# Two buffers outside the stages of a hybrid encoder block, in place of address pads

## The chip, the cores and the metric

The kernel runs on one core of a Trainium2 chip. The metric is the time of one execution on the device, in microseconds; several executions are taken and their median is given. The profile is of one more execution.

## The reference

One layer of a streaming encoder, for 512 tokens of width 1024, in float32. Only what the kernel's order of work needs is shown:

```python
h = rms_norm(x, norm_mix)
u_pool, u_lru, q, k, v, g_logits = split(h @ w_in)      # 5 x 1024 columns, and 3 x 1024 gate logits
gates = sigmoid(g_logits + b_gate)                      # 3 branches
y_pool = pool_mixer(u_pool)     # windows 2, 4, 8, 16: mean minus token, a 256x256 map, a scale
y_lru  = rglru_mixer(u_lru)     # conv of width 4, two gates, a linear recurrence over tokens
y_sb   = stick_breaking_attention(rms_norm(q), rms_norm(k), v)   # 8 heads of 128, causal
merged = sum(gates[i] * (y_i @ w_branch[i]) for the three branches)
x  = x + merged @ w_out
h2 = rms_norm(x, norm_ffn)
x  = x + (silu(h2 @ w_ffn_gate) * (h2 @ w_ffn_up)) @ w_ffn_down     # 2816 columns
```

## The kernel before, in words

Every product is made of three TensorE matmuls on operands split in a high and a low part (high x high, high x low, low x high). A weight piece of 128 x 1024 is loaded into a `raw` buffer, copied by ScalarE to `whi` (line 141) and subtracted by VectorE to `wlo` (line 142); there are three buffers of each in the pool `wp`. `weights` keeps about three pieces made ahead, at a priority 200 ahead of the place where they are emitted (`AHEAD`). Large products are done as seven half-size products instead of eight, in the order 11, 12, S2, S1, S3, S4, 22 (`ORDER`, and `product`, line 321, with moving operands of 256 columns).

The work is written as Python closures that are handed out during the matmuls: `tick` (line 363) takes one task from the list `abg` (attention) and one from `bg` (the rest). `half_chunk` calls `tick` after every twelve matmuls of a chunk. A planner then fixes the order on each engine from the order of emission, moved ahead by `tc.high_priority(n)`; each engine and each DMA queue (SP's, ACT's, and POOL's) works its list in order.

The stages that matter here, in order of time:

- **Start.** `warm` is filled with ones (line 335) and multiplied nine times (`WARM`, line 458) while the first loads arrive.
- **First stage** (pool `ap0`, tags `w`, `t` and `b` with 8, 8 and 13 buffers of 4 KB per partition): norm, gates of branches 0 and 1, the recurrence, then v, k, q (`tok_product`, line 837) which are stored by POOL's queue to DRAM (`qd`, line 790), then the gate of branch 2 as two units `cc` of seven products each (lines 894 to 920). A unit's two results `gx`, `gy` (line 895) are stored to `gd2` by POOL's queue (`gate_done`, line 892).
- **Mixing stage** (pools `sp`, `ap1`, `pmm`, `paux`): the pool `sp` takes the bytes of `ap0` and has 30 slots `s` and 12 slots `l` for loads, each 2 KB per partition. A tile waits for whatever last used its own bytes. `pmm` has three PSUM banks for chunk results, `paux` three for the attention and the pooling map.
  - Four pooling chunks in the order 1, 0, 3, 2 (`POOL`). Each leaves two banks, which ScalarE empties into slots (`evac_u`, line 981, results `up`). `pool_mean` (VectorE) and `pool_back` (TensorE, bank `pps`) follow as `bg` tasks, `pool_back` one chunk later.
  - Then four branch chunks of the recurrence (`ps_br`), then four of the pooling branch.
  - Beside these runs attention (`head_tasks`): for head h, `load` of q, k and v (`at`, line 1052, on SP's queue) at position 5h of `abg`, `trans` (eight transposes `pq`, line 1059, then copies `qkh`, `qkl`) at 5h+3, `vsplit` at 5h+4, three `scores` (`z`, `K`, `A`, `E`) at 5h+5, 5h+7 and 5h+9, `wtrans` (ten transposes `pw`, line 1109, in three banks, then `wth`, `wtl`) at 5h+12, and `yout` (`py`) at 5h+14.
- **Last branch, output product, FFN.** All with seven-product pieces except the first chunks; the products of `product` and of `piece` (line 1661) use moving operands of 256 columns.

Three things in the code of before are only about addresses. `PAD` is an unused tile of 41 floats. The `whi` and `wlo` buffers are 1152 floats long for a content of 1024, and a piece starts at an offset `o`: 0 for the pieces of ordinary chunks, and in the seven-product stages `STEPS` (0, 4, 8, 12) for the first four pieces and `OFF` (16) for all that follow. `warm` is as wide as the 512 columns that are multiplied.

```python
tx, ty = b4([2, S], f"gx{cc}"), b4([2, S], f"gy{cc}")     # tag "b"
...
def evac_u(ps, name):
    u = slot(name)
    act(two(u), in_order(ps), AF.Copy)
    return u
...
load_pool_weights(0)
queue_attention()
for g in POOL:
    pool_chunk(g)
```

Of the kernel before, what the change touches and what calls it, by code (L numbers as in the profile page):

```python
# [16 lines left out]
P = 128  # L17
S = 512
# [15 lines left out]
AHEAD = 200  # L34
PAD = 41


OFF = 16
STEPS = (0, 4, 8, 12)
NAW, NAT, NAB = 8, 8, 13  # L40
# [27 lines left out]
def layer_kernel(ctx: ExitStack, tc: tile.TileContext, x, xt, vecs, w_in, w_qkv7, w_gate7, w_pool, w_rg, w_ig,  # L68
# [6 lines left out]
    mp = ctx.enter_context(tc.tile_pool(name="mp", bufs=4))  # L75
    wp = ctx.enter_context(tc.tile_pool(name="wp", bufs=3))
    late = ctx.enter_context(ExitStack())
    hstack = ctx.enter_context(ExitStack())
# [50 lines left out]

    def weight_tiles(nh, nl, o=0):  # L130
        return [wp.tile([P, 1024 + 128], F32R, tag=tag, name=n)[:, o:o + 1024]
                for tag, n in (("whi", nh), ("wlo", nl))]

    def split_w(raw, shape, n, o=0):
        hi, lo = weight_tiles("whi" + n, "wlo" + n, o)
        if len(shape) == 3:
            hi, lo = (t.rearrange("p (a b) -> p a b", a=shape[1]) for t in (hi, lo))
        else:
            hi, lo = (t.rearrange("p (a b c) -> p a b c", a=shape[1], b=shape[2]) for t in (hi, lo))
        with tc.high_priority(60):  # L140
            act(hi, raw, AF.Copy)  # L141
            dve.tensor_tensor(lo, raw, hi.bitcast(F32), ALU.subtract)  # L142
        return hi, lo
# [58 lines left out]
    def add_seven(un, nm, i):  # L202
# [3 lines left out]
        def make(n):  # L206
            if nm == "S4":
                r = qraw[u, "12", i]
                dve.tensor_tensor(r, r, qraw[u, "S2", i], ALU.add)
            src = qraw[u, {"S1": "21", "S3": "11", "S4": "12"}.get(nm, nm), i]  # L210
            o = 0
            if u >= 3:
                o = goffs.pop(0) if goffs else OFF
            parts = split_w(src, [P] + list(shape), n, o)
            if nm == "11":
                qraw[u, "S2", i] = r = b4(list(shape), f"qs{u}{i}")
                dve.tensor_tensor(r, qraw[u, "21", i], src, ALU.add)
# [12 lines left out]
    goffs = list(STEPS)  # L230

# [28 lines left out]
    BNEXT = {"11": ("21", BY), "S1": ("11", BX), "S2": ("12", BX)}  # L260
    boffs = list(STEPS)

# [3 lines left out]
    def add_branch7(u, nm):  # L266
        def make(n):
# [3 lines left out]
            else:  # L271
                t = (BY if nm in ("11", "S3") else BX)[u]
            parts = split_w(t, [P, 2, 4, P], n, boffs.pop(0) if boffs else OFF)
            if nm in BNEXT:
# [57 lines left out]

    cst.tile([P, PAD], F32, tag="pad", name="pad")
    warm = cst.tile([P, S], BF16, tag="warm", name="warm")
    dve.memset(warm, 1.0)
# [108 lines left out]
    with ExitStack() as first:  # L444
# [12 lines left out]
        for i in range(WARM):  # L457
            nc.tensor.matmul(wps[:, 0, :], warm[:, 0:P], warm, start=True, stop=True)

# [434 lines left out]
        for cc in range(2):  # L894
            tx, ty = b4([2, S], f"gx{cc}"), b4([2, S], f"gy{cc}")
            if cc:
# [48 lines left out]
    with ExitStack() as mix:  # L945
# [34 lines left out]

        def evac_u(ps, name):
            u = slot(name)
            act(two(u), in_order(ps), AF.Copy)  # L983
            return u
# [35 lines left out]
        def pool_chunk(g):  # L1020
            pss = chan_chunk(("pool", g), hn, 1)
            us = [evac_u(pss[j], f"up{g}{j}") for j in range(2)]
            for j in range(2):
# [20 lines left out]
        def head_tasks(h):  # L1044
# [4 lines left out]
            def load():  # L1049
                for t in range(3):  # L1050
                    r = slot_ld(f"at{h}{t}", (NS, HD))
                    nc.sync.dma_start(r, qd[t, g][:, hd].rearrange("(b p) c -> p b c", p=P))
                    st["raw", t] = r
# [119 lines left out]
        def queue_attention():  # L1173
# [8 lines left out]
            for p in range(max(todo) + 1):  # L1182
                abg.append(lambda fs=todo.get(p, ()): [f() for f in fs])

        load_pool_weights(0)
        queue_attention()
        for g in POOL:
# [110 lines left out]
    with ExitStack() as ffn:  # L1298
# [114 lines left out]
        made = [0, NDIRECT]  # L1413
        offs = []

# [13 lines left out]
        def make_a(upto):  # L1429
            while made[0] < min(upto, len(steps)):  # L1430
                c, nm = steps[made[0]]
                made[0] += 1
                if (c, nm) == (NDIRECT, "11"):
                    offs.extend(STEPS)
                while made[1] < min(c + 2, DOWN):
# [5 lines left out]
        def split_a(src, n):  # L1441
            o = offs.pop(0) if offs else OFF
            h, l = (t.rearrange("p (w k c) -> p w k c", w=2, k=4)
                    for t in weight_tiles("wh" + n, "wl" + n, o))
            act(h, src, AF.Copy)  # L1445
# [133 lines left out]
        def make_d(upto):  # L1579
            while dmade[0] < min(upto, len(dsets)):  # L1580
                nm, n = dsets[dmade[0]]
                dmade[0] += 1
                if dmade[0] == 1:
                    offs.extend(STEPS)
                dfetch(dmade[0])
# [156 lines left out]
```

## Time and profile before

| What | us |
|---|---|
| median of 3 timed runs | 871.64 |
| lowest and highest of them | 871.51, 872.29 |
| the profiled execution, its own time | 872.32 |
| its span, first to last instruction | 870.5 |
| TensorE busy | 860.6 |
| VectorE busy | 741.1 |
| ScalarE busy | 523.1 |
| GpSimd busy | 91.2 |

The mean granted TensorE clock is 1.000. A row of the timeline has the start, the length (both in us, from the start of the span), the engine (a q behind it means the engine's queue, which issues), the line, the operation, what is written and read, the shapes and the count; in brackets stands how long the engine was idle before it and what released it. PE is TensorE, DVE VectorE, ACT ScalarE, POOL GpSimd, SP SyncE. A row of the waits has the total, the number of times and the longest.

### The profile page before, as it was taken

The page shows a single profiled execution, that of the slowest core. Times are in us where ns is not written, and L with a number is a line of the kernel's source. Part 1 is how long each engine was busy: PE and PEld are TensorE (multiplying, and loading weights), DVE is VectorE, ACT ScalarE, POOL GpSimd, SP SyncE. Part 2 cuts the span into 40 slices and gives each one's busy share as a digit, 9 for nine tenths or more (in the row PEclk, how much of TensorE's full clock was granted, in tenths as well). Part 3 has the DMA queues.
Part 4 walks back from the last instruction along what each step waited for, and adds up shares of the span by engine and source line. Part 5 has one row for each costly group of instructions (what it writes and reads, how often), then busy time and mean ns, then how long its engine had stood idle before and what let it go on. Part 6 is the DMA issues. An engine that isn't in the chain of part 4 may idle for free.

```text
span 870.5 us, 14271 instructions
## 1 busy us (share of the span) xinstructions
PE 860.6 (99%) x5563; PEld 790.0 (91%) x5563; DVE 741.1 (85%) x961; ACT 523.1 (60%) x727; POOL 91.2 (10%) x130
## 2 busy tenths in 40 slices
PE   9999999999999999999999999999999999999998
PEld 7888878888899888889889998889999999999998
DVE  7899897998796599977988786699998888899974
ACT  7554989557966565565665545464555555755642
POOL 1110002232433101000001100000000000121200
PEclk9999999999999999999999999999999999999999
DMA  9586356798582886644636955345543433797913
GB/s 339 165 287 203 98 167 187 212 324 253 178 275 73 241 243 203 221 122 151 214 103 167 199 172 169 98 139 151 156 111 97 116 104 119 228 240 194 196 42 121
DMA packets 116643, 154.08 MB, mean 177 GB/s; under 512 B 8160, under 2 KB 90080, under 8 KB 116576
## 3 DMA queue, kind: packets, MB, share of 16 engines
q1 hardware_dynamic: 103904, 107.30, 38.4%
q0 software_dynamic: 12528, 45.62, 22.0%
q8 instruction: 43, 0.70, 0.3%
q10 hardware_dynamic: 144, 0.26, 0.1%
q14 instruction: 24, 0.20, 0.1%
HBM read 132.71 MB, written 18.87 MB: 174 GB/s over the span
## 4 chain that ended last, share of the span: by engine, by line
PE 84%; DVE 7%; ACT 5%; DMA 2%; issue 1%; SPq 0%; ACTq 0%; DVEq 0%
PE ps_y L321 11%; PE ps_x L321 8%; PE ps_q L837 7%; PE ps_dy L1661 6%; PE ps_dx L1661 5%; PE ps_br L312 3%; PE ps_br L313 3%; PE ps_br L314 3%; PE ps_bY L1280 2%; PE ps_gate L740 2%; PE ps_gy L321 2%; DVE wlo L142 2%; PE ps_bX L1280 2%; PE ps_gx L321 2%; PE ps_lru L312 1%; PE ps_out L312 1%
## 5 line engine op out<-in xcount | busy, mean ns | idle before, releaser
L141 ACT ACTIVATE whi<-raw 128x1024 fp32r<-128x1024 f32 x69 | 72.9, 1056 | 78.3 <-PE ps_out L313 16.1
L142 DVE TENSOR_TENSOR wlo<-raw,whi 128x1024 fp32r<-128x1024 f32 x69 | 84.3, 1221 | 24.8 <-ACT whi L141 24.3
L142 DVE TENSOR_TENSOR wlo<-qw,whi 128x1024 fp32r<-128x1024 f32 x48 | 58.4, 1220 | 16.5 <-ACT whi L141 16.3
L141 ACT ACTIVATE whi<-qw 128x1024 fp32r<-128x1024 f32 x48 | 50.6, 1054 | 28.8 <-PE ps_q L837 14.8
L1445 ACT ACTIVATE wh_S<-w_S 128x1024 fp32r<-128x1024 f32 x36 | 38.2, 1062 | 30.2 <-PE ps_y L321 18.3
L1565 POOL DMA_DIRECT2D dw<-in_w_down_dram x20 | 17.0, 864 | 306.1 <-DMA dw<-in_w_down_dram 263.8
L1446 DVE TENSOR_TENSOR wl_S<-w_S,wh_S 128x1024 fp32r<-128x1024 f32 x36 | 43.9, 1221 | 3.2 <-ACT wh_S L1445 3.2
L1445 ACT ACTIVATE wh<-w 128x1024 fp32r<-128x1024 f32 x27 | 28.6, 1060 | 29.3 <-PE ps_x L321 9.1
L1446 DVE TENSOR_TENSOR wl<-w,wh 128x1024 fp32r<-128x1024 f32 x27 | 33.0, 1221 | 8.2 <-ACT wh L1445 8.2
L1445 ACT ACTIVATE whdS<-dw 128x1024 fp32r<-128x1024 f32 x20 | 21.2, 1061 | 20.3 <-PE ps_dy L1661 11.2
L1096 DVE TENSOR_TENSOR_SCAN E<-K,ahead 128x512 f32<-128x512 f32 (+3 forms) x32 | 25.4, 814 | 3.9 <-ACT K L1092 3.9
L1446 DVE TENSOR_TENSOR wldS<-dw,whdS 128x1024 fp32r<-128x1024 f32 x20 | 24.2, 1222 | 4.9 <-ACT whdS L1445 4.9
L312 PE MATMUL ps_br<-yHH,whi 128*128 128x512 f32 x64 | 24.6, 385 | 1.4 <-ACT up L983 1.4
L312 PE MATMUL ps_lru<-HH,whi 128*128 128x512 f32 x64 | 24.6, 384 | 0.0
L312 PE MATMUL ps_br<-yph,whi 128*128 128x512 f32 x64 | 24.5, 383 | 0.0
L312 PE MATMUL ps_pool<-HH,whi 128*128 128x512 f32 x64 | 24.5, 383 | 0.0
L312 PE MATMUL ps_gate<-HH,whi 128*128 128x512 f32 x64 | 24.4, 381 | 0.0
L313 PE MATMUL ps_lru<-HL,whi 128*128 128x512 f32 x64 | 24.3, 379 | 0.0
L314 PE MATMUL ps_lru<-HH,wlo 128*128 128x512 f32 x64 | 24.3, 379 | 0.0
L313 PE MATMUL ps_gate<-HL,whi 128*128 128x512 f32 x64 | 24.3, 379 | 0.0
L314 PE MATMUL ps_gate<-HH,wlo 128*128 128x512 f32 x64 | 24.3, 379 | 0.0
L313 PE MATMUL ps_pool<-HL,whi 128*128 128x512 f32 x64 | 24.3, 379 | 0.0
(740 smaller groups left out, 3444.5 us busy)
## 6 DMA issues: line engine op xcount, KB each, us to landing
raw<-in_w_in_dram SPq DMA_DIRECT2D x31, 512.0 KB, 5.3
qw<-in_w_qkv_dram SPq DMA_DIRECT2D x24, 512.0 KB, 6.8
dw<-in_w_down_dram POOLq DMA_DIRECT2D x20, 512.0 KB, 9.2
w<-in_w_ffn_gate_dram SPq DMA_DIRECT2D x36, 256.0 KB, 3.7
w<-in_w_ffn_up_dram SPq DMA_DIRECT2D x36, 256.0 KB, 4.2
raw<-in_w_branch_dram SPq DMA_DIRECT2D x16, 512.0 KB, 3.9
qw<-in_w_qkv_dram POOLq DMA_DIRECT2D x12, 512.0 KB, 8.1
qd<-r POOLq DMA_DIRECT2D x12, 512.0 KB, 6.7
```

The source lines that it names most:

```text
L141: act(hi, raw, AF.Copy)
L142: dve.tensor_tensor(lo, raw, hi.bitcast(F32), ALU.subtract)
L312: nc.tensor.matmul(ps, lh, rh, start=start, stop=False, skip_group_check=skip)
L313: nc.tensor.matmul(ps, lh, rl, start=False, stop=False, skip_group_check=skip)
L314: nc.tensor.matmul(ps, ll, rh, start=False, stop=stop, skip_group_check=skip)
L321: nc.tensor.matmul(o, a_[a][:, w, k, :], il2(b_[b][:, k, :]), start=first and n == k == 0, stop=last and n == 2 and k == 3, skip_group_che ...
L837: nc.tensor.matmul(ps[:, a, :], b_[:, k, ts_], il(a_[:, kk, :]), start=first and n == k == 0, stop=n == 2 and k == 3, skip_group_check=True)
L1096: dve.tensor_tensor_scan(E[:, c0:c0 + n][:, ::-1], K[:, c0 + 1:c0 + n + 1][:, ::-1], ahead[:, S - n:][:, ::-1], 0.0, ALU.mult, ALU.add)
L1280: nc.tensor.matmul(o, ah[x_][:, w, k, :], il2(b[k][y_]), start=first_ and n == k == 0, stop=n == 2 and k == 3, skip_group_check=True)
L1445: act(h, src, AF.Copy)
L1446: dve.tensor_tensor(l, src, h.bitcast(F32), ALU.subtract)
L1661: nc.tensor.matmul(o, a_[a][:, w, k0 + k, :], il2(b_[b][:, k, :]), start=first and i == k == 0, stop=last and i == 2 and k == nk - 1, skip ...
```

## The change

A pool `ex` with two buffers of 512 floats is opened beside `wp`, outside all stages. Head 0's q and k are loaded into them, at priority 400 ahead; later the last pooling chunk's two copies `up` use the same two buffers, at priority 300 ahead (`EARLY`). `queue_attention` now runs before `load_pool_weights(0)`, and the first task of its list, head 0's load, is taken off and run there; so each later attention task comes at one tick less. The second gate unit's `gx`, `gy` take buffers of tag `w` instead of `b`. `PAD`, `OFF` and `STEPS` go, the weight buffers are 1024 floats long and every piece starts at their beginning. `warm` has 128 columns and is read four times over by a broadcast.

```diff
+    ex = ctx.enter_context(tc.tile_pool(name="ex", bufs=2))
...
-    def weight_tiles(nh, nl, o=0):
-        return [wp.tile([P, 1024 + 128], F32R, tag=tag, name=n)[:, o:o + 1024]
+    def weight_tiles(nh, nl):
+        return [wp.tile([P, 1024], F32R, tag=tag, name=n)
...
-            o = 0
-            if u >= 3:
-                o = goffs.pop(0) if goffs else OFF
-            parts = split_w(src, [P] + list(shape), n, o)
+            parts = split_w(src, [P] + list(shape), n)
...
-            parts = split_w(t, [P, 2, 4, P], n, boffs.pop(0) if boffs else OFF)
+            parts = split_w(t, [P, 2, 4, P], n)
...
-    cst.tile([P, PAD], F32, tag="pad", name="pad")
-    warm = cst.tile([P, S], BF16, tag="warm", name="warm")
+    warm = cst.tile([P, P], BF16, tag="warm", name="warm")
...
-            nc.tensor.matmul(wps[:, 0, :], warm[:, 0:P], warm, start=True, stop=True)
+            nc.tensor.matmul(wps[:, 0, :], warm, warm.unsqueeze(1).to_broadcast([P, 4, P]), start=True, stop=True)
...
-            tx, ty = b4([2, S], f"gx{cc}"), b4([2, S], f"gy{cc}")
+            tx, ty = (b4([2, S], f"g{n}{cc}", "bw"[cc]) for n in "xy")
...
-        def evac_u(ps, name):
-            u = slot(name)
-            act(two(u), in_order(ps), AF.Copy)
+        def evac_u(ps, name, last):
+            u = ex.tile([P, S], F32, tag="u", name=name) if last else slot(name)
+            with tc.high_priority(EARLY if last else 0):
+                act(two(u), in_order(ps), AF.Copy)
             return u
...
-            us = [evac_u(pss[j], f"up{g}{j}") for j in range(2)]
+            us = [evac_u(pss[j], f"up{g}{j}", g == POOL[3]) for j in range(2)]
...
                 for t in range(3):
-                    r = slot_ld(f"at{h}{t}", (NS, HD))
-                    nc.sync.dma_start(r, qd[t, g][:, hd].rearrange("(b p) c -> p b c", p=P))
+                    with tc.high_priority(400 if h == 0 and t < 2 else 0):
+                        r = (ex.tile([P, NS, HD], F32, tag="u", name=f"at{h}{t}") if h == 0 and t < 2
+                             else slot_ld(f"at{h}{t}", (NS, HD)))
+                        nc.sync.dma_start(r, qd[t, g][:, hd].rearrange("(b p) c -> p b c", p=P))
...
-        load_pool_weights(0)
         queue_attention()
+        abg.pop(0)()
+        load_pool_weights(0)
         for g in POOL:
             pool_chunk(g)
...
-            o = offs.pop(0) if offs else OFF
             h, l = (t.rearrange("p (w k c) -> p w k c", w=2, k=4)
-                    for t in weight_tiles("wh" + n, "wl" + n, o))
+                    for t in weight_tiles("wh" + n, "wl" + n))
```

More of the change, by code (lines that the diff above doesn't have):

```diff
@@ L34 @@
 AHEAD = 200
-PAD = 41
-OFF = 16
-STEPS = (0, 4, 8, 12)
 NAW, NAT, NAB = 8, 8, 13
@@ L127, in halves, with split_w @@
         return [t[:, 0:2, :], t[:, 2:4, :]]
-    def weight_tiles(nh, nl, o=0):
-        return [wp.tile([P, 1024 + 128], F32R, tag=tag, name=n)[:, o:o + 1024]
+    def weight_tiles(nh, nl):
+        return [wp.tile([P, 1024], F32R, tag=tag, name=n)
                 for tag, n in (("whi", nh), ("wlo", nl))]
-    def split_w(raw, shape, n, o=0):
-        hi, lo = weight_tiles("whi" + n, "wlo" + n, o)
+    def split_w(raw, shape, n):
+        hi, lo = weight_tiles("whi" + n, "wlo" + n)
         if len(shape) == 3:
@@ L228, in add_seven @@
         specs.append((("seven", u, nm, i), make))
-    goffs = list(STEPS)
     def add_then(f):
@@ L260, in layer_kernel @@
     BNEXT = {"11": ("21", BY), "S1": ("11", BX), "S2": ("12", BX)}
-    boffs = list(STEPS)
     def bsrc(u, nm):
@@ L1183, in queue_attention @@
                 abg.append(lambda fs=todo.get(p, ()): [f() for f in fs])
+        queue_attention()
+        abg.pop(0)()
         load_pool_weights(0)
-        queue_attention()
         for g in POOL:
@@ L1413, in layer_kernel @@
         made = [0, NDIRECT]
-        offs = []
         def load_a(c):
@@ L1432, in make_a @@
                 made[0] += 1
-                if (c, nm) == (NDIRECT, "11"):
-                    offs.extend(STEPS)
                 while made[1] < min(c + 2, DOWN):
@@ L1582, in make_d @@
                 dmade[0] += 1
-                if dmade[0] == 1:
-                    offs.extend(STEPS)
                 dfetch(dmade[0])
```

## The prediction, made before the result

> **What bounds the kernel now.** The first view is the page's table of busy time: does one engine fill the span?
>
> ```profile
> span 870.5 us, 14271 instructions
> PE 860.6 (99%) x5563; PEld 790.0 (91%) x5563; DVE 741.1 (85%) x961; ACT 523.1 (60%) x727; POOL 91.2 (10%) x130
> ```
>
> TensorE (PE) is busy 860.6 of 870.5 us. So an edit can pay only where it takes away one of the few stretches in which PE waits, or costs where it makes a new one. The view of the waits, for PE alone, names them (total, times, longest):
>
> ```profile
> PE warm_ps L458 <- DVE warm L335: 1.5, 1, 1.5
> PE ps_br L312 <- ACT up L983: 1.4, 1, 1.4
> ...
> PE pq L1059 <- DMA at<-qd: 0.2, 1, 0.2
> ```
>
> The change touches three of these: the start (warm), the last pooling copies (up), and the first head's q and k (at). The second and the last lie in the mixing stage; the change reaches none of the causes of the longer waits left out here (the recurrence's and the q product's), which lie ahead of that stage.
>
> **The last pooling copies.** The timeline of PE and ACT around that wait:
>
> ```profile
> 341.06 0.38 PE L312 MATMUL ps_pool<-HH,whi 128*128 128x512 f32 x1
> ...
> 343.44 0.38 PE L314 MATMUL ps_pool<-HH,wlo 128*128 128x512 f32 x1
> ...
> 347.97 0.38 PE L314 MATMUL ps_br<-yHH,wlo 128*128 128x512 f32 x1
> 349.79 0.48 PE L312 MATMUL ps_br<-yHH,whi 128*128 128x512 f32 x1 [1.44 <-ACT up L983]
> ```
> ```profile
> 344.36 0.63 ACT L941 ACTIVATE p31h<-up 128x512 fp32r<-128x512 f32 x1 [3.55 <-DVE up L997]
> ...
> 349.12 1.10 ACT L983 ACTIVATE up<-ps_pool 128x512 f32<-128x512 f32 x2
> ```
>
> The twelve matmuls of the last chunk's second half run from 341.06 to 343.44, 0.216 us apart (2.38 / 11). The first of its two PSUM banks was complete before they began, the second is just after 343.44. ACT empties both only at 349.12, 0.55 us each, and the branch product that needs the first bank starts when that copy ends. From 347.97 to 349.79 are 1.82 us where one step is 0.216: **1.6 us lost**. ACT stood idle for 3.55 us before 344.36, so there is room: the first copy can run in it, the second would begin near 343.7. The change gives both copies buffers that no other slot user holds, and a priority 300 ahead. What it moves is 1.1 us of ACT work from 349 to about 340 to 345. Behind it wait p31h (until then at 344.36, later by at most 1.1 us) and, through it, DVE's subtraction p31l; the pooling product that reads them is queued only after the next chunk, at least four ticks of twelve matmuls or 10 us later, so I cost that at 0. Without that cover it costs the same 1.1 us. For this bank nothing is late next: the copy would be done by 344, and the branch product wants it at 348.2. I take **-1.6**, between 0 (the copies stay where they are in ACT's order) and -1.6.
>
> **The first head's q and k.** The same view at the first transposes, with those of a later head as a measure:
>
> ```profile
> 298.70 0.38 PE L314 MATMUL ps_pool<-HH,wlo 128*128 128x512 f32 x1
> 299.12 0.63 PE L1059 MATMUL pq<-idn,at 128*128 128x128 f32 x4
> 299.93 0.66 PE L1059 MATMUL pq<-idn,at 128*128 128x128 f32 x4 [0.18 <-DMA at<-qd]
> ...
> 334.16 1.04 PE L1059 MATMUL pq<-idn,at 128*128 128x128 f32 x8
> ```
>
> A later head's eight transposes take 1.04 us from the first's start to the last's end. The first head's take 1.47 (299.12 to 299.93 + 0.66), and they begin at 299.12, where PE was free for them at 298.92 (298.70 + 0.216): 0.43 + 0.20 = **0.6 us lost**, more than the 0.2 that the list of waits shows, since a pipeline that stops also has to refill. The cause is on the sync engine's queue:
>
> ```profile
> 243.27 3.72 SPq L198 DMA_DIRECT2D qw<-in_w_gate_dram  x2
> 285.63 6.35 SPq L148 DMA_DIRECT2D raw<-in_w_in_dram  x3
> 292.14 1.01 SPq L1052 DMA_DIRECT2D at<-qd  x2
> ```
> ```profile
> 253.93 0.75 POOL L790 DMA_DIRECT2D qd<-r  x1 [2.90 <-DVE r L854]
> ```
> ```profile
> at<-qd SPq DMA_DIRECT2D x7, 256.0 KB, 6.8
> ```
>
> The loads go out at 292.14, behind three weight loads, and land 6.8 us later, at 299. Their source is stored at 253.93; with the same time to land it is there at about 261. SP issues nothing from 247.0 to 285.6, so two loads into buffers that belong to no stage can go out at 261 and land near 268, and nothing queues behind them. Both issues (1.01 us) leave the place ahead of v's load, which then goes out at about 292 and lands at 299, for an ACT copy that PE needs ten ticks later. I take **-0.6**; the bounds are -0.6 and 0.
>
> **Attention a tick earlier.** The first task is now taken off the list before the pooling chunks, so every later attention task runs one tick earlier against the pooling and branch chunks: 12 x 0.216 = 2.6 us. No instruction is added, but the partners in each tick change: the weights' transposes of head 0 (three auxiliary banks) fall on tick 12, where a pooling product wants a bank too. What that can cost is bounded by two places:
>
> ```profile
> 329.66 1.25 PE L1109 MATMUL pw<-idn,A 128*128 128x128 f32 x10
> ```
> ```profile
> 332.24 1.61 DVE L1112 TENSOR_TENSOR wtl<-pw,wth 128x512 fp32r<-128x512 f32 x3
> ```
> ```profile
> 374.90 1.26 PE L1109 MATMUL pw<-idn,A 128*128 128x128 f32 x10
> ...
> 376.91 0.48 PE L312 MATMUL pps<-p20h,wph 128*128 128x512 f32 x1
> ```
>
> At 329.66 the banks come free when DVE has read them, the first at 332.24 + 1.61/3 = 332.8, some 2.1 us after the transposes; a product with nothing put ahead of it would wait that long. At 374.90 the same neighbours stand with scores between them and no wait is shown: 0. Earlier attention can also end one of the two small waits that remain in this stage, worth up to 0.5. I take **0**, nearest to the place that already has this neighbourhood, and keep -0.5 and +2.1.
>
> **Pads, offsets, gate buffers.** The pads free 6 x 512 + 164 + 768 = 4004 bytes of a partition for two buffers of 2048. Do they steer TensorE's pace? The products of the gates use offsets 0, 4, 8, 12 for their first four pieces and 16 after that; the first seven-product piece of the FFN has 0 again (chain of waits, merged):
>
> ```profile
> 251.20 2.68 PE ps_gy L321 x24
> ...
> 261.92 2.68 PE ps_gy L321 x24
> ...
> 593.27 2.68 PE ps_y L321 x24
> ```
>
> 24 matmuls take 2.68 us at offset 0 (251.20 and 593.27) and at 16 (261.92), 111.7 ns each. I take 0. Nothing is to be gained here, since this pace is the same everywhere; above, see the rival. The second gate pair now lies in weight buffers whose contents were split before its first copy; 0, and at most one piece, 2.7 us, if a buffer came free a piece late.
>
> **The start.** The broadcast operand keeps nine matmuls of 512 columns; only the fill shrinks.
>
> ```profile
> 0.92 0.48 DVE L335 MEMSET warm<- 128x512 bf16 x1 [0.92 <-PEq L1708]
> 1.46 4.02 PE L458 MATMUL warm_ps<-warm 128*128 128x512 bf16 x9 [1.46 <-DVE warm L335]
> 4.61 0.72 ACT L473 ACTIVATE hu<-xt,vt 128x512 fp32r<-128x512 f32 x1 [1.82 <-DMA xt<-in_xt_dram]
> 5.38 1.62 PE L740 MATMUL ps_gate<-hu,whi 128*128 128x512 f32 x4
> 6.83 1.03 PE L740 MATMUL ps_gate<-hu,wlo 128*128 128x512 f32 x4
> ```
>
> A fill of a quarter the size ends up to 0.3 us sooner, and so does the warm-up; but the first real matmul waits for ACT's 4.61 + 0.72 = 5.33 and stays at 5.38. The gain is 0. The step halves from about 430 ns (4.02 us for nine) to 216 (1.03 us for four, the last 0.38 long) between the second and the last row, at about 6.2, 4.7 us after PE began. The Trainium skill ("TensorE: Matmul & The Clock Gate", Part 1) has the clock open after a free-running window of about 3.4 us of sustained work; by it a start 0.3 us sooner moves nothing, and a window missed because of a longer pause would cost 1.7 us. The trace agrees with the delay's size but cannot show the window.
>
> **Sum.** -1.6 - 0.6 = -2.2 us. The profiled execution took 872.32 (span 870.5 and 1.8 around it), which gives 870.1; it lies 0.7 above the median of the three timed runs, 871.64, and against that median I forecast **869.4**. Its own range is 868.6 (the small waits and the start gain too) to 869.9.
>
> **Rivals.**
> 1. The wait moves: the auxiliary banks hold PE once for most of 2.1 us. For it: the 2.1 us come from a place where DVE was that late. Against: the neighbours at 374.90. 869.4 + 1.5 = 870.9. Chance 0.14.
> 2. The change does not do what it says: the up copies are held by ACT's order and not by a slot, and stay late. For it: no idle time stands before 349.12. Against: ACT's 3.55 us idle, which the priority reaches. Only 0.6 is won: 871.0. Chance 0.07.
> 3. The pause before 5.38 grows by 0.3 us and the clock counts anew from 5.38: it would open at 10.1, not 6.2, with 3.9 us at half pace, +1.95: 871.4. Chance 0.05.
> 4. Slower: without offsets, stationary and moving operands collide. The place is every 256-column product (91 pieces of 24 at L321 and L1280, and 840 at L1661: 3,024). It decides from (873.4 - 869.4) / 3,024 = 1.3 ns a matmul; at 2% (2.2 ns) it costs 6.8 us: 876. For it: in the changed kernel all pieces have equal offsets, where 16 was the rule. Against: the rows with 0 above. Chance 0.12.
> 5. Rival 1 in full at two ticks, 12 and 22: 869.4 + 4.2 = 873.6. Chance 0.06.
>
> The forecast keeps 0.56. **How the numbers follow.** A measurement of this kernel can tell about 0.2%, 1.74 us, from no change: faster means under 869.9, slower over 873.4. Faster 0.57 (the forecast and rival 1 at its small end), same 0.25 (rivals 1 to 3), slower 0.18 (4 and 5). The range 868.6 to 872.4 holds the forecast and rivals 1 to 3, two of them together included, and leaves out 4 and 5.
>
> **What would show it.** Right: the list of PE's waits has no ps_br on up and no pq on at; two loads of at stand on SP's queue near 261; up follows 343.5 on ACT; the first pq comes about 2.6 us sooner. Wrong: a wait of pps or pw on wtl near 327; up still behind yph; pieces of L321 above 2.68; a gate product at over 400 ns after 6.4.

## The result and the profile after

The changed kernel took **876.38 us** (median of six, 874.75 to 877.2) against 871.58 for the kernel before on the same chip (median of six, 871.01 to 872.31): a ratio of 1.0051, 95% interval 1.0039 to 1.0064. It is 4.8 us slower, where 2.2 us less were forecast. Its profiled execution took 877.2 us.

The page of the changed kernel, its first line and the engines' busy time:

```profile
span 875.4 us, 14270 instructions
PE 861.9 (98%) x5563; PEld 791.2 (90%) x5563; DVE 741.9 (85%) x961; ACT 522.0 (60%) x727; POOL 91.0 (10%) x130
```

The span is 4.9 us longer, and TensorE's busy time only 1.3: most of the loss is waiting. The waits of PE in the changed kernel (total, times, longest):

```profile
PE pw L1103 <- DVE ypl L1003: 4.2, 3, 2.0
...
PE pq L1053 <- DVE wtl L1106: 1.1, 1, 1.1
PE warm_ps L449 <- DVE warm L326: 1.1, 1, 1.1
```

The two waits that the change aimed at, `ps_br` on `up` and `pq` on `at`, are gone from the list. Two others stand there: the transposes `pw` wait three times for VectorE's `ypl` (the low part of the pooled map), and one `pq` waits for VectorE's `wtl`. The timeline of PE in the changed kernel shows where:

```profile
235.72 0.48 PE L828 MATMUL ps_q<-whi,hT3h 128*128 128x512 f32 x1 [0.45 <-ACT r L841]
...
296.65 1.04 PE L1053 MATMUL pq<-idn,at 128*128 128x128 f32 x8
...
326.65 0.55 PE L1103 MATMUL pw<-idn,A 128*128 128x128 f32 x3 [0.26 <-DVE ypl L1003]
...
341.69 0.38 PE L306 MATMUL pps<-p01h,wpl 128*128 128x512 f32 x1
...
348.38 0.60 PE L1103 MATMUL pw<-idn,A 128*128 128x128 f32 x4
...
349.64 0.38 PE L304 MATMUL ps_br<-yHH,whi 128*128 128x512 f32 x1
351.98 0.52 PE L1103 MATMUL pw<-idn,A 128*128 128x128 f32 x3 [1.96 <-DVE ypl L1003]
...
372.01 0.36 PE L304 MATMUL z<-qkh,qkh 128*128 128x256 f32 x1
374.38 0.55 PE L1103 MATMUL pw<-idn,A 128*128 128x128 f32 x3 [2.01 <-DVE ypl L1003]
...
376.38 0.63 PE L305 MATMUL ps_br<-yHL,whi 128*128 128x512 f32 x1
376.80 0.63 PE L306 MATMUL ps_br<-yHH,wlo 128*128 128x512 f32 x1
...
435.92 1.12 PE L1053 MATMUL pq<-idn,at 128*128 128x128 f32 x8 [1.12 <-DVE wtl L1106]
...
562.12 0.50 PE L1348 MATMUL ps_rms<-sqh,onesr 128*128 128x512 f32 x1
```

The first head's transposes now take 1.04 us like a later head's (296.65), so its q and k are in time. From 349.64 to 351.98 are 2.34 us where one step is 0.216: 2.1 lost. From 372.01 to 374.38, where one step of 256 columns would be 0.11, 2.3 are lost, and behind it the matmuls go 0.42 us apart (376.38 to 376.80), half pace, until 378.9: seven steps with 0.21 us too many, 1.5 us. At 435.92, `pq` has waited 1.12 us. With the 0.3 at 326 these losses come to 7.2 us; less the 2.2 us of the two stalls that are gone, 5.0 are left, near the 4.9 of the span.

Why the transposes wait is read on ScalarE and VectorE. The timeline of ACT in the changed kernel, then that of DVE:

```profile
345.44 0.58 ACT L975 ACTIVATE up<-ps_pool 128x512 f32<-128x512 f32 x1
349.82 0.63 ACT L932 ACTIVATE p31h<-up 128x512 fp32r<-128x512 f32 x1 [3.79 <-DVE up L989]
350.35 0.67 ACT L1002 ACTIVATE yph<-pps,vt 128x512 fp32r<-128x512 f32 x1
```
```profile
349.09 0.69 DVE L989 SCALAR_TENSOR_TENSOR up<-pw,up 128x512 f32<-128x512 f32 x1
350.48 0.69 DVE L933 TENSOR_TENSOR p31l<-up,p31h 128x512 fp32r<-128x512 f32 x1 [0.69 <-ACT p31h L932]
351.09 0.74 DVE L1003 SCALAR_TENSOR_TENSOR ypl<-pps,vt,yph 128x512 fp32r<-128x512 f32 x1
```

The pooling map's first product `pps` is complete at 341.9 (341.69 and a step of 0.216). Its bank comes free when VectorE has made `ypl`, at 351.09 + 0.74 = 351.83, 9.9 us later. ScalarE's part, `yph`, stands in its list behind `p31h`, which waits 3.79 us for VectorE's pooled mean. Ten transposes go in three groups of 4, 3 and 3, each to a bank of its own. The second group wants the bank at 348.74 (348.38 and four transposes, 0.36 in all), 6.8 us after the product: 3 us too soon, of which scores and one branch matmul cover 1.1. The rows of PE before, with the two points from which the table below counts, and the one of DVE before that frees this bank:

```profile
235.40 0.48 PE L837 MATMUL ps_q<-whi,hT3h 128*128 128x512 f32 x1 [0.46 <-ACT r L850]
...
340.85 0.38 PE L314 MATMUL pps<-p01h,wpl 128*128 128x512 f32 x1
...
352.48 1.26 PE L1109 MATMUL pw<-idn,A 128*128 128x128 f32 x10
...
356.99 1.03 PE L1059 MATMUL pq<-idn,at 128*128 128x128 f32 x8
...
556.65 0.50 PE L1353 MATMUL ps_rms<-sqh,onesr 128*128 128x512 f32 x1
```
```profile
348.11 0.74 DVE L1011 SCALAR_TENSOR_TENSOR ypl<-pps,vt,yph 128x512 fp32r<-128x512 f32 x1
```

Before, the bank was wanted 11.8 us after the product (352.84 less 341.07) and free after 7.8 (348.85); that it is the second group there too is taken from the order in which the three banks are handed out, the profile does not name them. The changed kernel takes 5.0 us from the first figure (a tick of 2.6 us, the pause of 1.6 on `up`, and 0.8 by which the product itself stands later) and adds 2.1 to the second.

### The profile page after: what moved, and what is told of

The parts are those of the page before. It is cut to its first block, busy times and chain, and to the rows that moved or that the text cites. A ratio compares the mean times of both kernels' runs of the same rounds, so it can differ in the third digit from the quotient of the medians.

```text
span 875.4 us, 14270 instructions
## 1 busy us (share of the span) xinstructions
PE 861.9 (98%) x5563; PEld 791.2 (90%) x5563; DVE 741.9 (85%) x961; ACT 522.0 (60%) x727; POOL 91.0 (10%) x130
## 4 chain that ended last, share of the span: by engine, by line
PE 57%; DVE 4%; ACT 1%; issue 1%; DVEq 0%; ACTq 0%
PE ps_y L313 11%; PE ps_x L313 8%; PE ps_dy L1650 6%; PE ps_dx L1650 5%; PE ps_br L305 3%; PE ps_br L306 3%; PE ps_br L304 3%; PE ps_bY L1275 2%; PE ps_bX L1275 2%; PE ps_out L304 1%; PE ps_out L306 1%; PE ps_out L305 1%; PE pw L1103 1%; PE ps_fu L306 1%; PE ps_fu L305 1%; PE ps_fu L304 1%
## 5 line engine op out<-in xcount | busy, mean ns | idle before, releaser
L305 PE MATMUL ps_br<-yHL,whi 128*128 128x512 f32 x64 | 24.9, 388 | 0.0
L306 PE MATMUL ps_br<-yHH,wlo 128*128 128x512 f32 x64 | 24.8, 388 | 0.0
L1086 ACT ACTIVATE K<-z,qrs 128x512 f32<-128x512 f32 (+3 forms) x32 | 17.0, 530 | 12.8 <-PE z L306 12.6
L305 PE MATMUL ps_br<-ypl,whi 128*128 128x512 f32 x64 | 24.3, 380 | 0.0
```

What stands on the lines that cost most here:

```text
L305: nc.tensor.matmul(ps, lh, rl, start=False, stop=False, skip_group_check=skip)
L306: nc.tensor.matmul(ps, ll, rh, start=False, stop=stop, skip_group_check=skip)
L1086: act(two(K[:, cs], 64), zs, AF.Sigmoid, scale=qrs[:, 1, i, h:h + 1])
```

## The experiments

Two questions. Does the attention's earlier tick cost all of it, and through what: VectorE's time (**theory T**) or the order of the users of the banks by itself (**rival P**)? And what are the two early loads and copies worth by themselves: do the `up` copies bring their 1.6 us, or does VectorE give them back (**theory D**)?

Beside the timed ratio to the kernel before on the same chip (95% interval) the table has the length of one stretch of each profiled execution, read as in the rows above: from the `ps_q` matmul near 235 that ends the last wait of the first stage, to `ps_rms` near 556. It holds the whole mixing stage and leaves out the start, whose length differs between executions of the same code.

| kernel | median us | ratio | stretch us |
|---|---|---|---|
| before | 871.58 | | 321.25 |
| changed | 876.38 | 1.0051 (1.0039 to 1.0064) | 326.40 |
| e1_tick_kept | 871.34 | 1.0002 (0.9993 to 1.0010) | 321.16 |
| e2_up_in_slots | 873.94 | 1.0039 (1.0026 to 1.0052) | 324.14 |
| e3_pads_alone | 871.49 | 0.9999 (0.9990 to 1.0008) | 321.23 |
| e4_map_copies_first | 876.13 | 1.0056 (1.0043 to 1.0068) | 326.36 |
| e6_qk_alone | 870.83 | 0.9991 (0.9982 to 0.9999) | 320.62 |
| e7_map_weights_early | 876.81 | 1.0057 (1.0045 to 1.0070) | 327.44 |
| e8_before_map_weights_early | 875.66 | 1.0044 (1.0031 to 1.0057) | 326.11 |
| e9_tick_later | 874.63 | 1.0032 (1.0020 to 1.0044) | 324.86 |
| e10_wpl_on_pool | 871.35 | 0.9997 (0.9988 to 1.0006) | 321.38 |
| e11_changed_relieved | 879.96 | 1.0095 (1.0081 to 1.0109) | 330.92 |
| e12_both_on_pool | 873.20 | 1.0019 (1.0010 to 1.0027) | 323.02 |
| e13_up_alone | 872.00 | 1.0007 (0.9998 to 1.0016) | 322.25 |
| e14_wpl_left_out | 870.47 | 0.9986 (0.9977 to 0.9995) | 320.38 |
| e15_changed_left_out | 871.66 | 1.0002 (0.9993 to 1.0011) | 321.73 |
| e16_means_later | 872.19 | 1.0007 (0.9998 to 1.0016) | 322.14 |
| e17_before_means_later | 873.74 | 1.0026 (1.0016 to 1.0036) | 323.32 |
| e18_mean_left_out | 869.32 | 0.9976 (0.9967 to 0.9986) | 319.34 |
| e19_mean_one_tick | 871.30 | 0.9999 (0.9990 to 1.0008) | 321.14 |

### The tick put back

```diff
         abg.pop(0)()
+        abg.insert(0, nothing)
```

> The changed kernel with one empty task put back at the head of the attention list, so that head 0's load is still taken off early but every other attention task runs at its old tick. Theory A (attention one tick earlier makes the new waits of pw on ypl): they go, the waits of ps_br on up and of the first pq on its loads stay away, 869.5 to 870.5 us. Theory B (the moved up copies make them, by pushing the pooling map's copies back on ACT and DVE): they stay, 874 to 877. Theory C (the missing pads and offsets): 876, whatever the ticks.

Theory A of this text holds that the earlier tick makes the waits, in whichever of the two ways, T or P; B blames the moved copies, C the missing pads. The whole loss is gone: 5.24 us less in the stretch than in the changed kernel, nothing left against the kernel before. So B and C fall as the cause of it. The time, 871.34, is still 0.8 above theory A's range: the 2.2 us of the two gains are missing. With the early loads and copies still in place, the waits of `pw` are gone, and a new one has come. PE and DVE in this kernel:

```profile
354.27 0.38 PE L306 MATMUL ps_br<-yHH,wlo 128*128 128x512 f32 x1
355.77 1.12 PE L1053 MATMUL pq<-idn,at 128*128 128x128 f32 x8 [1.12 <-DVE wtl L1106]
```
```profile
346.27 1.23 DVE L140 TENSOR_TENSOR wlo<-raw,whi 128x1024 fp32r<-128x1024 f32 x1 [0.74 <-ACT whi L139]
...
351.65 0.14 DVE L983 COPY pw<-up 128x1 f32<-128x1 f32 x1
...
353.90 1.22 DVE L140 TENSOR_TENSOR wlo<-raw,whi 128x1024 fp32r<-128x1024 f32 x1
355.03 1.61 DVE L1106 TENSOR_TENSOR wtl<-pw,wth 128x512 fp32r<-128x512 f32 x3
```

From 346.27 to 357 no row of VectorE has idle time before it, and `wtl`, which frees the bank for `pq`, stands near the end of that series. In the kernel before, the series starts at 346.97 and reaches `wtl` at 355.73, both 0.70 later; there TensorE lost 1.6 us on `up` first and then found the bank free. So TensorE gained 1.6 at 348 and VectorE hardly anything: the wait moved from ScalarE's `up` to VectorE's `wtl`.

### Other ticks, other parts alone

In e2 the tick is early and the `up` copies are in ordinary slots; in e9 the attention is a tick later than before; e6 is e1 without the `up` copies' part (q and k early alone), and e13 is e1 without the early q and k (`up` alone).

```diff
# e2, and e6 on top of e1
-            u = ex.tile([P, S], F32, tag="u", name=name) if last else slot(name)
-            with tc.high_priority(EARLY if last else 0):
-                act(two(u), in_order(ps), AF.Copy)
+            u = slot(name)
+            act(two(u), in_order(ps), AF.Copy)
# e9
+        abg[0:0] = [nothing, nothing]
# e13, on the changed kernel; the attention is back at its old ticks
+                        r = slot_ld(f"at{h}{t}", (NS, HD))
...
+        load_pool_weights(0)
         queue_attention()
-        abg.pop(0)()
-        load_pool_weights(0)
```

> The changed kernel with the last pooling copies back in ordinary slots and at ordinary priority; attention stays one tick earlier, q and k of head 0 stay early. A: the waits of pw on ypl stay (about 4 us), and the wait of ps_br on up comes back in part: 876 to 878 us. B: the waits of pw on ypl go, 871 to 872.5. C: 876.

> The changed kernel with two empty tasks put in, so that attention runs one tick later than in the kernel before. Theory T (attention ahead of its tick takes VectorE's time from the pooling means, whose map's copies then hold the auxiliary banks): later attention does the reverse, no wait of pw on ypl, 870.5 to 872 us. Rival P (the partners in a tick are what counts, and any move of one tick brings bank waits): 873 to 876.

> Attention at its old ticks, q and k of head 0 in the two outside buffers, the last pooling copies in ordinary slots at ordinary priority. Theory D (VectorE is the bound from about 346 to 357, so the 1.6 us that the up copies won are given back there): the loads' 0.6 us are kept, the wait of ps_br on up is back with 1.4 us and the wait of pq on wtl is gone: 870.6 to 870.9 us. Rival R (the first head's 0.6 us are given back too): 871.3.

> Attention at its old ticks, head 0's loads in ordinary slots as before, only the last pooling copies in the outside buffers with their priority; no pads. D: the wait of ps_br on up (1.4) goes, a wait of pq on wtl of 1.1 and two small ones come: 871.3 to 871.9 us, no gain. R (what is given back belongs to the early q and k): 869.9 to 870.2.

The first wait of e2, of e9, of e6 and of e13, in this order, from the lists of PE's waits:

```profile
PE pw L1102 <- DVE ypl L1002: 2.4, 2, 2.0
```
```profile
PE py L304 <- DVE qkl L1057: 3.8, 2, 2.0
```
```profile
PE ps_br L304 <- ACT up L974: 1.4, 1, 1.4
```
```profile
PE pq L1052 <- DVE wtl L1105: 1.7, 2, 1.5
```

A tick earlier costs without the early `up` copies too: e2 and e6 differ in the tick alone, and e2 is 3.52 us longer in the stretch. With the early copies the same tick costs 5.24: the wait near 372, 2.0 us with half pace behind it in the changed kernel, is 0.5 us in e2. The time of e2, 873.94, lies between what A and B expected of it. A tick later costs as well: e9 is 3.70 us longer than e1, with another pair of neighbours (`py` waits where VectorE's `qkl` is late). There theory T's forecast missed, and the time lies in rival P's range: both moves by one tick bring waits for banks. So the tick is not bad because it is early: the old one is the one of the three in which each bank's next user comes late enough. q and k alone win 0.63 us in the stretch and 0.09% (0.01 to 0.18) in time; the median and the ratio of e6 are the lowest of the kernels that compute everything. `up` alone wins nothing (872.00, a ratio of 1.0007, and 1.0 us more in the stretch): `ps_br` no longer waits, `pq` waits instead, 1.5 us for `wtl`, and 0.7 for its late loads.

### The pads

```diff
# before, with these edits only
-OFF = 16
-STEPS = (0, 4, 8, 12)
+OFF = 0
+STEPS = (0, 0, 0, 0)
...
-    cst.tile([P, PAD], F32, tag="pad", name="pad")
...
-        return [wp.tile([P, 1024 + 128], F32R, tag=tag, name=n)[:, o:o + 1024]
+        return [wp.tile([P, 1024], F32R, tag=tag, name=n)
```

> The kernel before without the unused tile and with weight buffers of 1024 floats, every piece at offset 0; warm and all else as before. A and B: 871.6 us, within 0.5, with 24 matmuls of a product in 2.68 us. C: 874 to 876, with more than 2.68 us for a piece.

The chain of waits of this kernel shows a piece of 24 at the pace of before:

```profile
250.77 2.68 PE ps_gy L320 x24
```

With a ratio of 0.9999 (0.9990 to 1.0008) the pads and offsets are worth nothing here.

### Does the earlier tick cost through VectorE?

The first trial gave the map's copies a higher priority:

```diff
# e4, on the changed kernel
+            with tc.high_priority(EARLY):
                 act(two(yh), in_order(ps), AF.Copy, scale=sc)
                 dve.scalar_tensor_tensor(two(yl), ...)
```

> The changed kernel with the two copies that empty the pooling map's bank (yph on ACT, ypl on DVE) at priority 300 ahead. If PE's wait of pw on ypl is a matter of their place in the two engines' order: both waits of 2 us go, 871.5 to 873 us. If DVE simply has no time by then (theory A with DVE as the bound): the wait shows under another name and the time stays at 875 to 877. C: 876.

The order on ScalarE and VectorE stayed as it was, so e4 says nothing on the cause. Two more (e7 on e1, e8 on before) moved the second load of the map's weights to the start of the stage:

```diff
-                bg.append(lambda: load_pool_weights(1))
+                bg.append(nothing)
...
+        load_pool_weights(1)
```

> The kernel with attention at its old ticks, and the second load of the pooling map's weights (two copies on ACT, two subtractions of 0.64 us on VectorE, which stand at 350.4 in that kernel) moved ahead of the pooling chunks, where VectorE idles. D: the wait of pq on wtl near 354 shrinks by 1.1 us or more, 869.8 to 870.3 us. R (the order of the copies makes the wait, not VectorE's time): 871.3.

> The kernel before with the same load moved, nothing else. D: VectorE's relief alone gives nothing while the branch product waits for the up copies on ACT: 871.3, within 0.3. If it gives 1 us or more, the relief and not the buffers would be what counts in the run with both.

The early load took a `raw` buffer that a chunk's weights needed, and a new wait came with it (4.2 us on `up` near 301 in e7, 3.3 us of `pq` on `at` near 300 in e8). In e7 the wait of `pq` on `wtl` did shrink to 0.2 us, but behind the new wait, in which VectorE can catch up; so neither run decides the question. What did was to take work off VectorE and give it to no other engine:

```diff
# e15, on the changed kernel
-                dve.tensor_tensor(lo, r, hi.bitcast(F32), ALU.subtract)
+                if h == 0:
+                    dve.tensor_tensor(lo, r, hi.bitcast(F32), ALU.subtract)
+                else:
+                    lo = hi
...
-                dve.tensor_tensor(b, st["raw", 2], a.bitcast(F32), ALU.subtract)
-                st["v"] = a, b
+                st["v"] = a, a
```

> The changed kernel, attention a tick early, with VectorE's low parts of v and of the second half of the map weights left out (the high parts stand in their place, so v and a part of the map product are not the reference's). Theory T (the tick shift costs because VectorE has not yet made the low parts of the pooled map when the transposes want the banks): both waits of the transposes for the low part of the map, 2.0 to 2.2 us each, shrink by the work that is gone, 0.6 to 1.9 us, the slow stretch of matmuls behind the second goes, and the time is 872 to 875. Rival P (the order of the bank's users alone): both waits stay at 2 and the time at 876.

The timeline of PE in this kernel, the two places:

```profile
348.87 1.11 PE L1105 MATMUL pw<-idn,A 128*128 128x128 f32 x6 [0.78 <-DVE ypl L1007]
...
370.71 1.21 PE L1105 MATMUL pw<-idn,A 128*128 128x128 f32 x6 [0.25 <-DVE ypl L1007]
```

The waits fall from 1.96 and 2.01 to 0.78 and 0.25 us, no slow matmuls follow, and the time falls to 871.66, below what theory T expected. TensorE's instructions are the same in number and size. So most of what the earlier tick costs comes of VectorE's being late there, and rival P, that the order alone does it, has fallen. Not all of it: e14 below has the old tick and a part of the same relief, and its stretch is 1.35 us shorter than e15's. That it takes both, a near user and a late VectorE, is what e1 and e15 show together.

### Does VectorE give the `up` copies' gain back?

The first way to relieve VectorE was GpSimd: the map weights' low parts there in e10 (on e1), these and v's low part in e12 (on e1) and in e11 (on the changed kernel).

```diff
-                dve.tensor_tensor(lo, r, hi.bitcast(F32), ALU.subtract)
+                nc.gpsimd.tensor_tensor(lo, r, hi.bitcast(F32), ALU.subtract)
# e11 and e12 also
-                dve.tensor_tensor(b, st["raw", 2], a.bitcast(F32), ALU.subtract)
+                nc.gpsimd.tensor_tensor(b, st["raw", 2], a.bitcast(F32), ALU.subtract)
```

> Attention at its old ticks, both outside buffers used as in the changed kernel, and the four subtractions of the pooling map's weights given to GpSimd instead of VectorE (two of them, 1.29 us, stand on VectorE ahead of the copies wtl for which PE waits at 354). Theory D (VectorE's time gives the 1.6 us back): the wait of pq on wtl goes from 1.1 us to 0.2 or less, 869.8 to 870.5 us. Rival R (a wait that does not hang on VectorE's load): 871.3, the wait stays.

> The changed kernel, attention one tick early, with the subtractions of the pooling map's weights and of v given to GpSimd. Theory T with D (VectorE is late with the pooling means because attention took its time): the two waits of pw on ypl of 2 us shrink by the 0.7 to 2 us of VectorE's work that is gone ahead of each, 872 to 874.5 us. Rival P (the partners in a tick alone): both stay at 2 us, 876.

> As the first of these runs, with the subtraction of v on GpSimd too (0.69 us of VectorE for each head). D: at or below that run, 869.3 to 870.3 us, the small waits near 353 and 361 (0.3 us each) gone as well. If GpSimd's longer subtraction makes a wait of its own (py on vl), more than that run.

GpSimd and VectorE in e10, around the moved subtractions:

```profile
349.33 2.98 POOL L969 TENSOR_TENSOR wpl<-rawp,wph 128x512 fp32r<-128x512 f32 x2 [4.31 <-ACT wph L968]
```
```profile
350.02 1.14 DVE L1092 TENSOR_TENSOR A<-A,E 128x512 f32<-128x512 f32 x1
...
351.15 1.70 DVE L984 TENSOR_TENSOR pw<-up 128x511 f32<-128x511 f32 x1
...
352.96 0.68 DVE L984 TENSOR_TENSOR pw<-pw 128x510 f32<-128x510 f32 x1
```

While GpSimd works (349.33 to 352.31), two of VectorE's two-input operations take 1.14 and 1.70 us, where the same ones take 0.68 in e1 and right behind it: 1.48 us more, where 1.29 had been moved away. The wait stayed (1.2 us). The Trainium skill ("SBUF — State Buffer", "Who interferes with whom") says that a VectorE instruction with two SBUF inputs contends with a GpSimd instruction that reads SBUF; the trace agrees, with these numbers. So e10 did not test the theory: it swapped one load on VectorE for another. e11 and e12, with more moved to GpSimd, are longer in the stretch than the kernels they were made from, by 4.5 and 1.9 us; in e11 the three waits of `pw` on `ypl` come to 6.5 us, where they were 4.2.

Next, the low part was left out in e1 (as in e15's first edit), and the mean's order was changed, in e16 on e1 and in e17 on before:

```diff
# e16, e17
+            if g == POOL[3]:
+                queue_pool_back(POOL[2])
             for j in range(2):
                 bg.append(lambda j=j, u=us[j]: pool_mean(g, j, u))
-            if g != POOL[0]:
+            if g in POOL[1:3]:
```

> The changed kernel with the attention at its old ticks, and with one thing left out: the low parts of the second half of the map weights are not computed (two VectorE subtractions of 0.64 us each, 1.29 together, gone), and the high parts stand in their place in the matmuls, so that part of the product is not the reference's. Theory D (the 1.6 us that the early up copies win are given back because VectorE is the bound from 346 to 357): the wait of the queries' matmuls for VectorE's copy of the transposed weights near 354, 1.1 us in the kernel with the old ticks, shrinks to 0.2 us or less, and the time to 869.9 to 870.4. Rival (the wait hangs on banks or on ScalarE): it stays at 1.0 or more and the time at 871.3.

> The changed kernel with the attention at its old ticks, computing everything, with one reordering: the pooled mean of the last pooling chunk is queued behind the pooled-back work of the chunk before it. Theory D: VectorE reaches its copy of the transposed weights before the long chain of the mean, the wait of the queries' matmuls near 354 goes from 1.1 to 0.3 us or less, and the time to 869.9 to 870.5. Rival: the mean turns late for the pooled scores or the wait moves to another consumer, and the time stays at 871.3 or goes above.

> The kernel before with only that reordering of the mean. Theory D: nothing is won while the branch product's banks still wait 1.5 us for the up copies, 871.3 to 871.9. Rival (the reordering alone is the gain, whatever the up copies do): 870.0 to 870.6.

In e14 the time fell (0.78 us in the stretch against e1), but the named wait did not. PE and DVE in e14:

```profile
355.42 1.12 PE L1057 MATMUL pq<-idn,at 128*128 128x128 f32 x8 [1.24 <-DVE wtl L1110]
```
```profile
352.73 0.17 DVE L991 SCALAR_TENSOR_TENSOR pw<-pw,invpos 128x7 f32<-128x7 f32 x1
352.94 0.69 DVE L993 SCALAR_TENSOR_TENSOR up<-pw,up 128x512 f32<-128x512 f32 x1
...
354.68 1.61 DVE L1110 TENSOR_TENSOR wtl<-pw,wth 128x512 fp32r<-128x512 f32 x3
```

The time that became free was filled: the mean's last two instructions, behind `wtl` in e1, now stand ahead of it, and `wtl` is only 0.35 us earlier. In e16 and e17 the pooled-back products moved two ticks too. In e16 the wait of `pq` near 354 is gone, but one of these products waits 1.0 us for a bank that `wtl` holds and another 0.8 us for `p20h`, which is made from the mean that now comes later; e17 has such a wait for `p20h` of 0.7 beside the old one on `up`. Their stretches are longer by 1.0 us (than e1's) and 2.1 us (than that of before). All three left the theory open, since more than the one thing moved. So the last two runs kept TensorE's order around the copy:

```diff
# e18, on e1: no mean for the last chunk's first half
-            while sh < w:
+            while sh < w and (g, j) != (POOL[3], 0):
...
+            if (g, j) != (POOL[3], 0):
                 dve.scalar_tensor_tensor(prev[:, 0:w - 1], ...)
                 dve.scalar_tensor_tensor(u, prev, 1.0 / w, u, ALU.mult, ALU.subtract)
# e19, on e1: both means one tick later, pooled-back products at their ticks
+            if g == POOL[3]:
+                bg.append(nothing)
...
+                    m = bg.pop()
+                    bg.append(lambda: (m(), pool_back(p, 0)))
+                    bg.append(lambda: pool_back(p, 1))
```

> The changed kernel with the attention at its old ticks, and with the pooled mean of the last chunk's first half left out (the copied chunk itself is split in its place, so that a quarter of the pooled map is not the reference's). TensorE's order is unchanged; on VectorE six instructions (2.25 us in the kernel with the old ticks, from 351.65 to 353.90) no longer stand ahead of its copy of the transposed weights, and one of 0.6 us moves there, so that the copy comes 1.65 us earlier. Theory D (VectorE's chain up to that copy gives the 1.6 us back): the wait of the queries' matmuls, 1.1 us, goes to 0.2 or less, the 0.3 us losses at 352.8 and 361.4 may stay, and the time is 869.6 to 870.3. Rival (another thing holds these matmuls): the wait stays at 0.8 or more and the time is 871.0 to 871.4.

> The changed kernel with the attention at its old ticks, computing everything: the two pooled means of the last chunk run one tick later, the pooled-back products stay at their ticks. Theory D: VectorE's copy of the transposed weights stands 2.25 us earlier in its order, the wait of the queries' matmuls near 354 goes, and if nothing else comes late, 869.7 to 870.4. Rival: the delayed means make the pooled-back products of the last chunk wait 1 to 2 us near 380, the gain is given back a third time and the time is 871.0 to 872.5.

PE and DVE in e18:

```profile
354.22 0.38 PE L306 MATMUL ps_br<-yHH,wlo 128*128 128x512 f32 x1
354.44 1.04 PE L1054 MATMUL pq<-idn,at 128*128 128x128 f32 x8
```
```profile
351.56 0.69 DVE L933 TENSOR_TENSOR p20l<-up,p20h 128x512 fp32r<-128x512 f32 x1
...
353.30 1.61 DVE L1107 TENSOR_TENSOR wtl<-pw,wth 128x512 fp32r<-128x512 f32 x3
```

`wtl` starts 1.73 us earlier than in e1, `pq` follows at once, and the time is 869.32, some 2.1 us under the kernel before, as the forecast's sum had it (2.2). Theory D holds: both gains were real, and VectorE's work ahead of `wtl` gave the larger back. The kernel before with the same mean left out was not run. Its rows leave little room for a gain by the relief alone: that mean begins at 352.35 there, behind the end of TensorE's wait on `up` at 349.79, and `wtl` cost it 0.2 us. In e19, which computes everything, `pq` does not wait either, and the list of waits shows what does:

```profile
PE pps L304 <- ACT p21h L932: 1.5, 1, 1.5
```

The later means make the last pooled-back product wait, and the 1.6 us are given back a third time. I found no order in which they stay won.

## Why the prediction was wrong

- **What bounds it.** Right for TensorE as a whole. Not seen: VectorE, at 85% of the span, has no row with idle time between 346.97 and 360.5 of the kernel before, so in this stretch it is the second limit. The share of the whole span hid that.
- **The last pooling copies, -1.6.** The size and the mechanism were right; the wait went, and e18 shows the gain. The step that failed is "nothing is late next": it was said of that bank alone, and the next bank, freed by VectorE's `wtl`, was late by 1.1 us. In before, `wtl` ends its first third near 356.3 and `pq` comes at 356.99; moved 1.6 us earlier, `pq` would have come at 355.4. The rows for that sum were there. So the sum's -2.2 was worth 0.1 with the old ticks (e1's stretch against that of before).
- **The first head's q and k, -0.6.** Right: e6 has -0.63 in the stretch.
- **Attention a tick earlier, 0.** This step failed, by 5.24 us (the changed kernel against e1). It chose between two places that looked alike, one that loses 2.1 us and one that loses nothing, and took the second. Neither was the right measure. What decides is how long after the product the transposes want its bank (11.8 us before, 6.8 after) against how long VectorE and ScalarE take to free it (7.8 and 9.9). The prediction also had the wait the wrong way round: it looked for a product that waits for a bank of the transposes (`wtl`), and the transposes waited for the product's bank (`ypl`). The pieces of the loss are 0.3 at 326, 2.1 and 2.3 at the other two `pw` waits, 1.5 of half pace, and 1.1 of `pq` at 435.
- **Pads 0.** Right (e3). The slow rival for them (4) is refuted. **Gate buffers 0:** not tried alone; e1 carries them and ends level with before.
- **The start, 0.** 0.1 us later at the first real matmul (5.47), 0.3 at 235, within what executions of the same code differ by. The prediction read the 4.7 us until the pace doubles as agreeing with a window of about 3.4; the last section has 2.7 and 8.4 us for one start, so that agreement says little.
- **The rivals.** Rivals 1 and 5 named the banks and the 2.1 us a time; two such waits came. One is head 2's, at tick 22 as rival 5 had it; the other is head 1's, and at tick 12, head 0's, only 0.3 us were lost. Rivals 2 and 3 did not come: the copies moved, and the doubled pace came near 7.0 us, not at 10.1. Rival 5's price, 873.6, left out the half pace behind the second wait and the wait at 434, and the holder was the map's `ypl` rather than `wtl`. Its chance of 0.06 was far too low: nothing in the profile spoke against it but one place with other neighbours.

## What to carry to other kernels

When a step is moved in a kernel whose buffers are shared, take for each buffer the time between its last writer and its next user, before and after the move, and compare it with how long the releasing engine's list takes there; a place that merely looks alike is no bound. A wait that goes uncovers the next one, so work out the next user's release before counting the whole stall as won. An engine at 85% over the span can be at 100% in the one stretch that matters: look at its idle times in that stretch.

## What the runs showed of the hardware

**The clock drops after a short wait.** In the changed kernel 2.0 us of waiting at 372 were followed by matmuls 0.42 us apart until 378.9, and the granted clock is 0.50 from 375.65 to 379.05; a wait of the same length at 349.64 was not followed by any slow step. In e9 the second of two waits of 2 us was followed by slow steps, too (granted clock 0.50 from 371.6 to 374.9), and in e7 a wait of 4.2 us by some 6.8 us at 0.50. Of the ten single waits between 1.8 and 2.6 us here (two each in the changed kernel, e4 and e9, one in e2, three in e11) four were followed by some 3.4 us at half clock. In e8 two waits of 1.8 and 1.5 us, one shortly behind the other, were followed by it as well. No single wait of 1.7 us or less had that consequence in any kernel here. The Trainium skill ("TensorE: Matmul & The Clock Gate", Part 1) has the clock close after an idle window of about 3.4 us; here 2.0 us sometimes sufficed, and the measurement decides.

**The start differs between executions of the same code.** The starts of e6 and of e1, whose instructions there are the same, from their timelines of PE:

```profile
5.78 2.08 PE L731 MATMUL ps_gate<-hu,whi 128*128 128x512 f32 x4 [0.70 <-ACT hu L464]
7.64 1.91 PE L731 MATMUL ps_gate<-hu,wlo 128*128 128x512 f32 x4
```
```profile
5.36 1.13 PE L731 MATMUL ps_gate<-hu,whi 128*128 128x512 f32 x4 [0.88 <-ACT hu L464]
```

Four matmuls take 2.08 us in the one and 1.13 in the other: in e6's profiled execution the clock opened some 8.4 us after TensorE began (1.06 to about 9.5), in e1's at about 3.75, 2.7 us after, during the nine warm-up matmuls. e6's profiled execution took 872.76 us against its median of 870.83. The Trainium skill (the same page and part) has the clock's window run free of the kernel, so that the point of opening varies by 500 ns either way; the traces agree that it varies, but by 5.7 us here, and the measurement decides. A profile's span alone would have shown e6 slower than before; the stretch that leaves the start out does not.
